# RG-LRU gates of a hybrid trunk: one 64-row product per 64-channel block in place of two zero-padded 128-row products

## The chip, the cores and the metric

One core of one Trainium2 chip runs the program. The metric is the device time of one execution in microseconds (us), as the median of several runs. PE is the matrix engine (TensorE), PEld its weight loads, ACT the ScalarE, DVE the VectorE, POOL the GpSimd engine, SP the engine whose queue issues most DMAs. Lnnn is a line of the kernel before.

## What is computed

Two layers of a streaming-encoder trunk over 256 tokens of width 1024. Each layer has a SwiGLU half-step, a mixer, a second SwiGLU half-step and an input embedding, each followed by a layer norm. The mixer projects x once and feeds three branches (RG-LRU, GLA, FoX). The change lies in the two gates of the RG-LRU branch, which has 512 channels in 8 blocks of 64:

```python
def rg_lru(x, wa, ba, wx, bx, lam):
    xb = xf.reshape(bsz, seq, LRU_BLOCKS, LRU_BLOCK)
    r = jax.nn.sigmoid(jnp.einsum('bsnc,ncd->bsnd', xb, wa.astype(f32)).reshape(bsz, seq, width) + ba.astype(f32))
    i = jax.nn.sigmoid(jnp.einsum('bsnc,ncd->bsnd', xb, wx.astype(f32)).reshape(bsz, seq, width) + bx.astype(f32))
    log_a = -LRU_C * r * jax.nn.softplus(-lam.astype(f32))
    a = jnp.exp(log_a)
    mult = jnp.sqrt(-jnp.expm1(2.0 * log_a))
    h = linear_scan(a, mult * (i * xf))
    return h.astype(x.dtype)
```

## The kernel before, in words

Weights stream from memory in pieces (`Weights.prefetch`, L183). For a piece the SP queue issues a DMA into `raw`, ACT rounds it into `whi` (L201) and DVE takes the rest into `wlo` (L202). Up to 8 pieces are held (`R_MAIN`), and a piece that PE has finished with is freed, which issues the next two. Every product with a streamed weight is three products of rounded parts (L305 to L307, L317 to L319).

All instructions are issued in the order of the program text, and each engine runs its own in that order. In the mixer (L527) the matrix units are run one after the other by `run` (L909): `run(unit, new chains)` first lets every chain in progress take one more step, up to its next `yield`, and then issues the unit's products. So the small chains of the three branches are laid between the units by hand:

- `run(lambda: unit_ay(1), lru(0))` starts `lru(0)`, the gates of the first 256 channels; `run(lambda: b_both(3, 1), lru(1))` starts `lru(1)`, those of the other 256.
- `unit_bq` and then `unit_cq(0)` follow. With `unit_cq(0)` the chain `gla_states` starts (products at L747, DVE copies at L756).
- Before `unit_k(0)` the chain `fox_forget` takes its transposes (L646), which read the tile `fcat` that DVE wrote at L634 to L639.
- Before `unit_cq(1)` the chain `gla_out` starts (products at L784, which read `gs`).

`lru(i)` (L684) does the gate products (L691), four sigmoids on ACT (L695), two tanh (L698) and two exp (L700), then `yield`s to its DVE steps. A tile of 256 channels stands on 128 partitions: column half `j` of `xc` holds 128 channels (two blocks) by 256 tokens. `wa` holds for each gate `w` and each pair of blocks a 128x128 matrix that is zero off its two 64x64 blocks. One PSUM tile (bank) holds one gate for both `j`. A float32 product is two passes on PE, each with its own weight load. There are 8 PSUM banks in one pool (`psp`), given out and given back in program order.

`gla_states` (L747), `gla_out` (L784) and `fox_attend` (L830) already use products of 64 rows, with the two halves in two banks.

Of the kernel before, what the change touches and what calls it, by code (L numbers as in the profile page):

```python
# [13 lines left out]
AF = mybir.ActivationFunctionType  # L14
# [3 lines left out]
P = 128  # L18
# [5 lines left out]
DEPTH = 2  # L24
# [116 lines left out]
V_CW, V_CB, V_BA, V_BX, V_LAM, NV = 0, 4, 5, 6, 7, 8  # L141


def constants():
    p = np.arange(P)
    ident = np.eye(P)
    suffix = (p[:, None] > p[None, :]) & (p[:, None] // 64 == p[None, :] // 64)
    prefix = p[:, None] <= p[None, :]
    ones = np.ones((P, P))
    chunk = p[:, None] // 64 == np.arange(2)[None, :]  # L150

    head = p[:, None] % 8 == np.arange(8)[None, :]
    keys, queries = p[:, None] < 24, (p[:, None] >= 32) & (p[:, None] < 56)
    cf = np.concatenate([ident, suffix, prefix, ones, chunk, head & queries, head & keys, -1.0 * keys, queries], 1).astype(np.float32)
    mask = np.where(p[None, :] <= p[:, None], 0.0, -1e30)
    cb = np.concatenate([ident, mask], 1).astype(np.float32)
    return cf, cb
# [74 lines left out]
def build(tc, a, out):  # L232
# [15 lines left out]
    def nm(s):  # L248
        count[0] += 1
        return f"{s}_{count[0]}"  # L250

    def ps():
        return psp.tile([P, 512], F32, tag="ps", name=nm("ps"))

    def work(n=512, dt=F32):
        return wk.tile([P, n], dt, tag="w", name=nm("w"))
# [4 lines left out]
    V, S, G, TE = nc.vector, nc.scalar, nc.gpsimd, nc.tensor  # L261

    def load(dst, src):
        nc.sync.dma_start(dst, src)

    def tt(out, in0, in1, op):
        return V.tensor_tensor(out=out, in0=in0, in1=in1, op=op)  # L267

    def stt(out, in0, scalar, in1, op0, op1):
        return V.scalar_tensor_tensor(out=out, in0=in0, scalar=scalar, in1=in1, op0=op0, op1=op1)  # L270
# [256 lines left out]
    def mixer(l, turn):  # L527
# [4 lines left out]
        wa = mt([P, 2, 4, P], F32, "wa")  # L532
# [3 lines left out]
        v = lambda kind, j: vec[:, (l * NV + kind) * 4 + j:(l * NV + kind) * 4 + j + 1]  # L536
# [22 lines left out]

        steps(b_steps((0, 1), 0), BT, turn, BA)  # L560
        W.hold = False
        load(wa, a["lru"][:, l])
        load(wg2, a["wg2"][l])
        load(ng, a["ng"][l, :].partition_broadcast(P))
        load(bf, a["bf"][l, :].partition_broadcast(P))
# [92 lines left out]
        def yt():  # L658
            y = mt([P, 4, 2, T], F32R, "y", 2)
            return y, y[:, :, 0, :], y[:, :, 1, :]  # L660


        ya = yt()
        js = [slice(j * T, (j + 1) * T) for j in range(2)]
# [19 lines left out]
        def lru(i):  # L684
            xc = lru_t["xc", i]
            r, ix, th = work(), work(), work()
            gates = []
            for w in range(2):
                o = ps()
                for j in range(2):  # L690
                    TE.matmul(o[:, js[j]], lhsT=wa[:, w, 2 * i + j, :], rhs=xc[:, js[j]], start=True, stop=True)  # L691
                gates.append(o)
            for w, dst in ((0, r), (1, ix)):
                for j in range(2):
                    S.activation(dst[:, js[j]], gates[w][:, js[j]], AF.Sigmoid, bias=v(V_BA + w, 2 * i + j))  # L695
            cs = [lruc[:, l * 4 + 2 * i + j:l * 4 + 2 * i + j + 1] for j in range(2)]
            for j in range(2):
                S.activation(th[:, js[j]], r[:, js[j]], AF.Tanh, scale=cs[j])  # L698
            for j in range(2):
                S.activation(r[:, js[j]], r[:, js[j]], AF.Exp, scale=cs[j])  # L700
            yield
            tt(ix, ix, xc, ALU.mult)

            tt(xc, r, r, ALU.mult)
            stt(th, xc, 1.0, th, ALU.add, ALU.mult)
            yield
            S.activation(th, th, AF.Sqrt, scale=-1.0)
            yield
            tt(ix, ix, th, ALU.mult)
            for j in range(2):  # L710
                V.tensor_tensor_scan(out=xc[:, js[j]], data0=r[:, js[j]], data1=ix[:, js[j]], initial=0.0, op0=ALU.mult, op1=ALU.add)
            tt(xc, xc, lru_t["ga", i], ALU.mult)
            yield
            hi, lo = (x[:, 2 * i:2 * i + 2, :] for x in ya[1:])
            xc3 = xc.rearrange("p (j c) -> p j c", j=2)
            S.activation(hi, xc3, AF.Copy)
            yield
            tt(lo, xc3, hi.bitcast(F32), ALU.subtract)
# [15 lines left out]


        yb = yt()
        rows = [slice(0, 64), slice(64, 128)]

        def gla_states():
            kd, dec = gla["kd"], gla["dec"]  # L740
# [174 lines left out]
        run(lambda: unit_ax(1), gla_decays())  # L915
        run(lambda: unit_ay(0), fox_forget(), gla_gate())
        run(lambda: unit_ay(1), lru(0))
        run(lambda: b_both(3, 0))
        run(lambda: b_both(3, 1), lru(1))
        run(unit_bq)  # L920
        run(lambda: unit_cq(0), gla_states())
# [182 lines left out]
    for l in range(DEPTH):  # L1104
        turn = ffn(l, 1, 0, hp, turn)
        W.close()
        sctx.close()
        gb, chains = mixer(l, turn)
        sctx, hp = open_scope(l + 1)
        turn = merge_out(l, gb, chains)  # L1110
        turn = ffn(l, 2, 2, hp, turn)
        turn = ple(l, turn, l == DEPTH - 1)
# [5 lines left out]
def lay_out(x, p, ffn1_w_up, ffn1_w_down, ln1_g, ln1_b, w_in, conv_w, conv_b, lru_wa, lru_ba, lru_wx, lru_bx,  # L1118
            lru_lambda, gla_w_g2, gla_b_g, gla_norm_g, fox_b_f, w_branch, w_out, ln2_g, ln2_b, ffn2_w_up,
            ffn2_w_down, ln3_g, ln3_b, ple_w_proj, ple_w_gate, ple_b_gate, ln4_g, ln4_b):  # L1120
    ws = {k: np.asarray(v) for k, v in locals().items()}
    f = np.float32
    parts = ((C_BK + 256, 512), (C_BK + 784, 512), (C_BK + 768, 16), (C_CF, 8), (C_BK, 256), (C_CV, 512))
    ws["tm"] = np.concatenate([ws["w_in"][..., c:c + n] for c, n in parts], -1)
    wu = np.empty(SIZE, f)
    for key, name, index, r0, rows, c0, cols, off in PIECES:
        block = ws[name][index][r0:r0 + rows]
        if "gu" in key[0]:
            block = np.concatenate([block[:, c0:c0 + 256], block[:, FF + c0:FF + c0 + 256]], -1)
        else:  # L1130
            block = block[:, c0:c0 + cols]
        block = block.reshape(rows // P, P, cols)
        wu[off:off + rows * cols].reshape(P, rows // P, cols)[...] = block.transpose(1, 0, 2)
    m = {"wu": wu}
    m["x"] = ws["x"].reshape(T, D)
    m["xT"] = ws["x"].reshape(T, KD, P).transpose(2, 1, 0).reshape(P, KD * T)
    m["pT"] = ws["p"].reshape(DEPTH, T, 2, P).transpose(3, 0, 2, 1)
    m["lnp"] = np.stack([ws[f"ln{i}_{c}"][l] for l in range(DEPTH) for i in range(1, 5) for c in "gb"])
    vec = np.empty((DEPTH, NV, 4, P), f)
    vec[:, :4] = ws["conv_w"].reshape(DEPTH, 4, 4, P)  # L1140
    for i, k in enumerate(("conv_b", "lru_ba", "lru_bx", "lru_lambda")):
        vec[:, 4 + i] = ws[k].reshape(DEPTH, 4, P)
    m["vec"] = vec.transpose(3, 0, 1, 2).reshape(P, DEPTH * NV * 4)
    lru = np.zeros((P, DEPTH, 2, 4, P), f)
    for w, k in enumerate(("lru_wa", "lru_wx")):
        for j in range(8):
            h = slice((j % 2) * 64, (j % 2) * 64 + 64)
            lru[h, :, w, j // 2, h] = ws[k][:, j].transpose(1, 0, 2)
    m["lru"] = lru
    wg2 = np.zeros((DEPTH, P, 256), f)  # L1150
    wg2[:, :16] = ws["gla_w_g2"]
    wg2[:, 32] = ws["gla_b_g"]
    m["wg2"] = wg2
    m["ng"] = ws["gla_norm_g"]
    m["bf"] = ws["fox_b_f"]
    m["bg"] = ws["ple_b_gate"]
    m["cf"], m["cb"] = constants()
    return {f"in_{k}": np.ascontiguousarray(v) for k, v in m.items()}
# [11 lines left out]
```

## Time and profile before

| | |
|---|---|
| median of 3 runs | 1316.31 us (1315.8 to 1317.02) |
| profiled execution | 1317.07 us, of which the span of its instructions is 1315.3 us |
| granted TensorE clock | 0.996 of full speed over the span |
| busy, share of the span | PE 98%, PEld 86%, DVE 68%, ACT 54%, POOL 4% |
| moved by DMA | 245.47 MB, mean 187 GB/s |

Busy shares are averages over stages with different limits. How a stage is bound is read from the time lines of its engines and from the table of waits, which says for each wait what ended it.

### The profile page before, as it was taken

To read this page: it belongs to the slowest core of one execution; us is meant where nothing else is said; L and a number is where in the kernel's file an instruction comes from. 1 tells how busy PE (TensorE), PEld (TensorE's weight loads), DVE (VectorE), ACT (ScalarE), POOL (GpSimd) and SP (SyncE) were. 2 spreads that over 40 slices of the span, in tenths; PEclk is the share of its full clock that TensorE was granted. 3 is DMA by queue.
4 is the path that set the end of the run, shared out by engine and by line. 5 is a ranking of instruction groups with operands and counts; after the bars stand their busy time and mean duration, and the time that the engine had idled before them with its cause. 6 is when DMAs were issued, how large, how long until landed. Compare 5 with 4: busy or idle time off the path is not lost. (4 is left out here: it accounts for less than half of the span.)

```text
span 1315.3 us, 19952 instructions
## 1 busy us (share of the span) xinstructions
PE 1287.2 (98%) x7892; PEld 1134.0 (86%) x7892; DVE 888.6 (68%) x1200; ACT 703.9 (54%) x1001; POOL 46.5 (4%) x42
## 2 busy tenths in 40 slices
PE   8999999999999999999999999999999999999996
PEld 7888888999999888887778888899999988888885
DVE  6776675678658666667776667665876586666676
ACT  6655545975445455554345556359655444555541
POOL 0000000000011000000000000000000110000000
PEclk9999999999999999999999999999999999999998
DMA  8865746446556465574555557463454655555731
GB/s 268 286 195 192 242 144 209 142 146 197 168 196 208 132 204 193 188 238 158 177 192 191 191 188 250 134 227 123 158 193 156 195 194 169 189 186 190 254 129 71
DMA packets 70061, 245.47 MB, mean 187 GB/s; under 512 B 8144, under 2 KB 8784, under 8 KB 69968
## 3 DMA queue, kind: packets, MB, share of 16 engines
q1 hardware_dynamic: 69680, 243.81, 56.2%
q8 instruction: 62, 1.02, 0.3%
q10 hardware_dynamic: 288, 0.39, 0.1%
q14 instruction: 31, 0.25, 0.1%
HBM read 243.12 MB, written 1.05 MB: 186 GB/s over the span
## 5 line engine op out<-in xcount | busy, mean ns | idle before, releaser
L202 DVE TENSOR_TENSOR wlo<-raw,whi 128x1024 fp32r<-128x1024 f32 (+2 forms) x442 | 538.6, 1228 | 252.5 <-ACT whi L201 251.3
L201 ACT ACTIVATE whi<-raw 128x1024 fp32r<-128x1024 f32 (+2 forms) x442 | 457.2, 1044 | 217.2 <-PE ps L318 80.7
L340 PE MATMUL ps<-XX,whi 128*128 128x512 f32 x1050 | 373.2, 393 | 0.0
L341 PE MATMUL ps<-XX,wlo 128*128 128x256 f32 x1200 | 312.5, 281 | 0.0
L341 PEld LDWEIGHTS ps<-XX,wlo 128*128 128x128 f32 x1200 | 226.0, 188 | 12.7 <-DVE wlo L202 0.2
L340 PEld LDWEIGHTS ps<-XX,whi 128*128 128x128 f32 x1050 | 196.9, 188 | 40.0
L317 PE MATMUL ps<-XX,whi 128*128 128x256 f32 x688 | 196.6, 286 | 5.9 <-ACT whi L201 5.9
L319 PE MATMUL ps<-XX,wlo 128*128 128x256 f32 x688 | 193.0, 281 | 0.0
L318 PE MATMUL ps<-XX,whi 128*128 128x256 f32 x688 | 193.0, 281 | 0.0
L305 PE MATMUL ps<-whi,hh 128*128 128x512 f32 x368 | 145.3, 395 | 2.5 <-ACT hh L276 2.5
L307 PE MATMUL ps<-whi,hl 128*128 128x512 f32 x368 | 144.1, 392 | 0.0
L306 PE MATMUL ps<-wlo,hh 128*128 128x512 f32 x368 | 143.2, 389 | 0.0
L345 ACT ACTIVATE w<-ps 128x256 f32<-128x256 f32 x150 | 57.3, 382 | 157.6 <-PE ps L343 157.6
L305 PE MATMUL ps<-whi,XX 128*128 128x512 f32 (+2 forms) x360 | 140.6, 391 | 0.0
L307 PE MATMUL ps<-whi,XX 128*128 128x512 f32 (+2 forms) x360 | 137.6, 382 | 1.1 <-DVE XX L267 1.1
L306 PE MATMUL ps<-wlo,XX 128*128 128x512 f32 (+2 forms) x360 | 137.5, 382 | 0.0
L317 PEld LDWEIGHTS ps<-XX,whi 128*128 128x128 f32 x688 | 130.3, 189 | 8.1 <-ACT whi L201 5.9
L318 PEld LDWEIGHTS ps<-XX,whi 128*128 128x128 f32 x688 | 130.4, 189 | 0.1
L319 PEld LDWEIGHTS ps<-XX,wlo 128*128 128x128 f32 x688 | 130.2, 189 | 0.2 <-DVE wlo L202 0.2
L267 DVE TENSOR_TENSOR w<-ps,w 128x256 f32<-128x256 f32 (+1 forms) x159 | 69.1, 435 | 76.4 <-ACT w L345 76.4
L307 PEld LDWEIGHTS ps<-whi,hl 128*128 128x128 f32 x368 | 69.0, 188 | 17.0 <-DVE hl L267 1.7
L305 PEld LDWEIGHTS ps<-whi,hh 128*128 128x128 f32 x368 | 69.1, 188 | 16.4 <-ACT hh L276 4.0
(171 smaller groups left out, 1371.1 us busy)
## 6 DMA issues: line engine op xcount, KB each, us to landing
raw<-in_wu SPq DMA_DIRECT2D x430, 512.0 KB, 4.2
gb<-in_lnp SPq DMA_DIRECT2D x16, 512.0 KB, 6.1
raw<-in_wu SPq DMA_DIRECT2D x8, 280.0 KB, 5.2
xr<-in_xT SPq DMA_DIRECT2D x4, 256.0 KB, 5.0
raw<-in_wu SPq DMA_DIRECT2D x4, 256.0 KB, 5.2
XR<-in_x SPq DMA_DIRECT2D x1, 1024.0 KB, 7.5
wa<-in_lru SPq DMA_DIRECT2D x2, 512.0 KB, 4.0
w<-in_bg SPq DMA_DIRECT2D x4, 256.0 KB, 5.0
```

The costliest lines, as they stand in the source:

```text
L201: self.nc.scalar.activation(hi[:, c], raw[:, c], AF.Copy)
L202: (lo or self.nc.vector).tensor_tensor(out=lw[:, c], in0=raw[:, c], in1=hi[:, c].bitcast(F32), op=ALU.subtract)
L267: return V.tensor_tensor(out=out, in0=in0, in1=in1, op=op)
L305: TE.matmul(o, lhsT=lh[:, k, c], rhs=hi[:, kk, :], start=start and kk == 0, stop=False)
L306: TE.matmul(o, lhsT=lh[:, k, c], rhs=lo[:, kk, :], start=False, stop=False)
L307: TE.matmul(o, lhsT=ll[:, k, c], rhs=hi[:, kk, :], start=False, stop=stop and kk == kt - 1)
L317: TE.matmul(o, lhsT=hi[:, kk, c], rhs=rhs[:, k, 0, :], start=start and kk == 0, stop=False)
L318: TE.matmul(o, lhsT=hi[:, kk, c], rhs=rhs[:, k, 1, :], start=False, stop=False)
L319: TE.matmul(o, lhsT=lo[:, kk, c], rhs=rhs[:, k, 0, :], start=False, stop=stop and kk == kt - 1)
L340: TE.matmul(o, lhsT=hi[:, k, :], rhs=both, start=k == 0, stop=False)
L341: TE.matmul(o[:, :T], lhsT=lo[:, k, :], rhs=XX[:, k, 0, :], start=False, stop=False)
L345: S.activation(lows[:, c], o[:, T:], AF.Copy)
```

## The change

Each 64-channel block now has its two 64x64 gate matrices side by side in one 64x128 matrix. For each column half `j` and each block `e` of it (even on partitions 0 to 63, odd on 64 to 127) one product contracts 64 rows and gives 128 outputs: gate r on PSUM partitions 0 to 63 and gate i on 64 to 127. Even blocks go to one bank, odd blocks to another. The products are four for one `lru` as before, but of 64 rows. Each sigmoid now covers 64 partitions, from `rows[w]` of bank `e` to `rows[e]` of the output, so there are eight of 64x256 where there were four of 128x256. The load of `wa` is half as large (its tile keeps its size, since `unit_k` uses the slot again), and `rows` is defined earlier.

```diff
-        load(wa, a["lru"][:, l])
+        load(wa[:, 0], a["lru"][:, l])
...
-            gates = []
-            for w in range(2):
-                o = ps()
-                for j in range(2):
-                    TE.matmul(o[:, js[j]], lhsT=wa[:, w, 2 * i + j, :], rhs=xc[:, js[j]], start=True, stop=True)
-                gates.append(o)
+            gates = [ps() for _ in range(2)]
+            for j in range(2):
+                for e in range(2):
+                    TE.matmul(gates[e][:, js[j]], lhsT=wa[rows[e], 0, 2 * i + j, :], rhs=xc[rows[e], js[j]], start=True, stop=True)
             for w, dst in ((0, r), (1, ix)):
                 for j in range(2):
-                    S.activation(dst[:, js[j]], gates[w][:, js[j]], AF.Sigmoid, bias=v(V_BA + w, 2 * i + j))
+                    for e in range(2):
+                        S.activation(dst[rows[e], js[j]], gates[e][rows[w], js[j]], AF.Sigmoid, bias=v(V_BA + w, 2 * i + j)[rows[e]])
...
-    lru = np.zeros((P, DEPTH, 2, 4, P), f)
+    lru = np.zeros((P, DEPTH, 4, P), f)
...
-            lru[h, :, w, j // 2, h] = ws[k][:, j].transpose(1, 0, 2)
+            lru[(j % 2) * 64:(j % 2) * 64 + 64, :, j // 2, w * 64:w * 64 + 64] = ws[k][:, j].transpose(1, 0, 2)
```

## Rows read from the trace of the kernel before

**Rows 1.** The page, its first part: busy time of the engines, share of the span, instructions.

```profile
PE 1287.2 (98%) x7892; PEld 1134.0 (86%) x7892; DVE 888.6 (68%) x1200; ACT 703.9 (54%) x1001; POOL 46.5 (4%) x42
```

**Rows 2.** The table of waits for PE alone, whole run: who waited for whom, us in total, times, longest.

```profile
PE ps L317 <- ACT whi L201: 5.9, 1, 5.9
...
PE ps L784 <- ACT whi L201: 2.6, 2, 1.3
...
PE ps L646 <- DVE fcat L639: 0.4, 2, 0.3
```

**Rows 3.** Windows: busy time of each engine in three stretches, with the granted clock and the DMA share. The first two are the stretch from the first `axp` copy to the `bq` copy in the mixer of layer 0 and of layer 1; the third follows it in layer 0.

```profile
core 0: us, PE busy (x) PEld busy (x) DVE busy (x) ACT busy (x) POOL busy (x), PEclk, DMA share, GB/s
235.40:276.50 41.10, 40.83 (x309) 37.62 (x308) 21.30 (x38) 40.71 (x57) 2.74 (x2) 1.00 0.38 117
887.50:929.50 42.00, 41.83 (x314) 38.52 (x313) 21.82 (x40) 41.60 (x57) 2.73 (x2) 1.00 0.36 119
276.50:285.10 8.60, 7.22 (x74) 6.52 (x76) 8.46 (x18) 4.93 (x6) 0.00 (x0) 1.00 0.37 124
```

**Rows 4.** Time line of ACT in layer 0: start, us, line, operation, count, and in brackets the idle time before it and what ended that.

```profile
234.37 1.06 ACT L201 ACTIVATE whi<-raw 128x1024 fp32r<-128x1024 f32 x1 [1.74 <-PE ps L318]
235.42 0.60 ACT L671 ACTIVATE axp<-ps 128x512 f32<-128x512 f32 x1
...
251.13 1.57 ACT L695 ACTIVATE w<-ps,vec 128x256 f32<-128x256 f32 x4
252.57 0.92 ACT L698 ACTIVATE w<-w,lruc 128x256 f32<-128x256 f32 x2
...
266.65 1.57 ACT L695 ACTIVATE w<-ps,vec 128x256 f32<-128x256 f32 x4
268.09 0.92 ACT L698 ACTIVATE w<-w,lruc 128x256 f32<-128x256 f32 x2
...
272.57 1.05 ACT L201 ACTIVATE whi<-raw 128x1024 fp32r<-128x1024 f32 x1
...
275.89 0.59 ACT L722 ACTIVATE bq<-ps 128x512 f32<-128x512 f32 x1
278.90 0.63 ACT L716 ACTIVATE y<-w 128x512 fp32r<-128x512 f32 x1 [2.42 <-DVE w L267]
```

**Rows 5.** Time line of DVE, the same columns: layer 0, and behind the last gap one row of layer 1.

```profile
264.75 0.69 DVE L267 TENSOR_TENSOR w<-w,tm 128x512 f32<-128x512 f32 x1
272.22 1.23 DVE L202 TENSOR_TENSOR wlo<-raw,whi 128x1024 fp32r<-128x1024 f32 x1 [6.78 <-ACT whi L201]
273.65 1.23 DVE L202 TENSOR_TENSOR wlo<-raw,whi 128x1024 fp32r<-128x1024 f32 x1 [0.20 <-ACT whi L201]
274.79 0.17 DVE L634 COPY s<-ps 128x16 f32<-128x16 f32 x1
...
276.07 0.17 DVE L639 CAST fcat<-s 128x16 bf16<-128x16 f32 x1
...
283.11 0.48 DVE L756 COPY gs<-ps 128x128 f32<-128x128 f32 x2
283.51 1.64 DVE L270 SCALAR_TENSOR_TENSOR gs<-gs,s,ps 128x128 f32<-128x128 f32 x6
...
926.71 1.23 DVE L202 TENSOR_TENSOR wlo<-raw,whi 128x1024 fp32r<-128x1024 f32 x1 [0.20 <-ACT whi L201]
```

**Rows 6.** Time line of PE around the transposes of `fcat`: layer 0, then layer 1.

```profile
275.74 0.28 PE L319 MATMUL ps<-XX,wlo 128*128 128x256 f32 x1
276.30 0.29 PE L646 MATMUL ps<-cb,fcat 128*128 128x128 bf16 x2 [0.27 <-DVE fcat L639]
...
929.36 0.28 PE L646 MATMUL ps<-cb,fcat 128*128 128x128 bf16 x2 [0.17 <-DVE fcat L639]
```

**Rows 7.** Groups of ACT instructions by line and shape (out<-in, count, busy us, mean ns of one).

```profile
L201 ACT ACTIVATE whi<-raw 128x1024 fp32r<-128x1024 f32 x430 | 449.3, 1055 | 211.0 <-PE ps L318 80.7 <-DMA raw<-in_wu 58.2 <-issue 28.3
...
L695 ACT ACTIVATE w<-ps,vec 128x256 f32<-128x256 f32 x16 | 6.3, 475 | 0.0
...
L578 ACT ACTIVATE w<-w 128x16 f32<-128x16 f32 x2 | 0.4, 216 | 0.0
```

**Rows 8.** Time line of PE around the gate products of `lru(0)` in layer 0 (the products take xc and wa; x8 are four products of two passes).

```profile
240.52 0.28 PE L318 MATMUL ps<-XX,whi 128*128 128x256 f32 x1
240.64 0.28 PE L319 MATMUL ps<-XX,wlo 128*128 128x256 f32 x1
240.75 1.89 PE L691 MATMUL ps<-w,wa 128*128 128x256 f32 x8
...
242.60 0.28 PE L318 MATMUL ps<-XX,whi 128*128 128x256 f32 x1
```

**Rows 9.** Time line of PE around the products of `gla_states` in layer 0 (16 float32 products of 64 rows and 64 columns, two passes each).

```profile
268.91 0.28 PE L319 MATMUL ps<-XX,wlo 128*128 128x256 f32 x1
...
269.12 1.10 PE L747 MATMUL ps<-gv,w 64*64 64x128 f32 x32
...
270.15 0.39 PE L317 MATMUL ps<-XX,whi 128*128 128x256 f32 x1
...
270.38 0.28 PE L318 MATMUL ps<-XX,whi 128*128 128x256 f32 x1
```

**Rows 10.** Time line of PE in `fox_attend` in layer 0: products of 64 rows and 128 columns, even and odd halves in two banks.

```profile
303.64 0.28 PE L830 MATMUL ps<-gv,qh 64*128 64x128 f32 x2
...
303.76 0.27 PE L830 MATMUL ps<-wa,ql 64*128 64x128 f32 x2
```

**Rows 11.** Windows of PE alone around one pause between the layers: us, busy time, granted clock (PEclk), DMA share.

```profile
652.24:655.65 3.41, 3.41 (x13) 0.50 0.28 84
648.80:652.24 3.44, 1.14 (x8) 1.00 0.47 155
```

**Rows 12.** The page, DMA issues: size and median us from issue to landing.

```profile
wa<-in_lru SPq DMA_DIRECT2D x2, 512.0 KB, 4.0
```

More of the change, by code (lines that the diff above doesn't have):

```diff
@@ L660, in yt @@
             return y, y[:, :, 0, :], y[:, :, 1, :]
+        rows = [slice(0, 64), slice(64, 128)]
         ya = yt()
@@ L736, in mixer @@
         yb = yt()
-        rows = [slice(0, 64), slice(64, 128)]
         def gla_states():
@@ L1143, in lay_out @@
     m["vec"] = vec.transpose(3, 0, 1, 2).reshape(P, DEPTH * NV * 4)
-    lru = np.zeros((P, DEPTH, 2, 4, P), f)
+    lru = np.zeros((P, DEPTH, 4, P), f)
     for w, k in enumerate(("lru_wa", "lru_wx")):
         for j in range(8):
-            h = slice((j % 2) * 64, (j % 2) * 64 + 64)
-            lru[h, :, w, j // 2, h] = ws[k][:, j].transpose(1, 0, 2)
+            lru[(j % 2) * 64:(j % 2) * 64 + 64, :, j // 2, w * 64:w * 64 + 64] = ws[k][:, j].transpose(1, 0, 2)
     m["lru"] = lru
```

## The prediction

> **What bounds the kernel now.** I read the page's busy times first: PE is busy for 1287.2 us of a span of 1315.3, so over the whole run the kernel is bound by products, and time that PE loses is not won back later [rows 1]. Taken alone this says that products should be cut. The second view, PE's waits, says what ends the little idle time that it has: after the start (5.9 us for the first weights) PE never waits long for a weight piece, but at two places in the mixer it waits for the small chains, at L646 for `fcat` from DVE and at L784 [rows 2]. Both lie shortly behind the changed lines, so I looked at that stretch by itself. In the 41.1 us from the first `axp` copy to the `bq` copy ACT is busy for 40.71 us, in layer 1 for 41.60 of 42.00, while DVE is busy for half of the time [rows 3]. ACT's average of 54% hides a stretch in which it is as full as PE.
>
> The time line of ACT shows how [rows 4]: from the copy at 235.42, which PE's product released, to the copy at 275.89 no idle time stands in brackets. Sigmoids, tanh, exp, table loads and the splitting of weights follow each other without a pause, and both `lru` calls lie in it (251.13 and 266.65). Nothing that ACT does there is waiting for PE: it works off a backlog. Now I follow who waits for the end of the backlog. DVE stands idle for 6.78 us and again for 0.20 us until ACT has split a weight piece (the one at 272.57 ends at 273.62; DVE starts at 273.65); in DVE's queue the `fcat` steps come right behind that piece, from 274.79 to 276.24 [rows 5]. PE issues its last product of `unit_cq(0)` at 275.74, could go on some 0.12 later, and starts L646 at 276.30 with idle time that `fcat` ends; in layer 1 the same happens at 929.36 [rows 6]. So the path that sets the time in this stretch is ACT's queue, then two DVE steps, then PE; PE reaches L646 about 0.4 us early in both layers.
>
> **The change part by part.** *Sigmoids.* Four instructions become eight in each `lru`. The elements per partition stay 256. An ACT row's time goes with those: 1055 ns for 1024, 475 for 256, 216 for 16 [rows 7]. No ACT row of this kernel covers fewer than 128 partitions, so the cost of a 64x256 sigmoid is bounded. From below: half the cost, which makes the eight as long as the four, +0; I see no reason for less, since the same elements are read. From above: 0.475 each with no overlap, 8 x 0.475 - 1.44 = +2.36 us for a call. Back to back, four take from 251.13 to 252.57, 1.44 us or 0.36 each [rows 4]. The nearest row is the sigmoid itself with half of the lanes idle, so I take the same 0.36: eight take 2.88, +1.44 us for a call. Two calls in a layer lie on the gap-free stretch, +2.88 us; two layers, **+5.76 us**.
>
> The Trainium skill, "ScalarE: Activation LUTs", section "What ACT_TABLE_LOAD costs", gives an activation with a pointer bias 280 ns + 0.833 ns for each element of a partition, less some 93 ns of overlap, with no term for partitions: an estimate of 0.40 us for each, +1.6 for a call and 6.4 in all. The row's 0.475 us and step of 0.36 are both below its 0.493 and 0.40, and the sum goes by the rows.
>
> *Who takes it up.* ACT has no gap in which to take it up, DVE's start at 273.65 is released by ACT, and PE's slack is 0.4 us but in the wrong place: PE waits for DVE already, so a later `fcat` moves L646 one for one, 276.30 to about 279.2. After that DVE is busy for 8.46 us of 8.60 up to the `gs` steps [rows 3], all behind `fcat` in its queue, so the start of L784, which waits for `gs` at 283.51 [rows 5], moves by the same 2.88. Weight pieces split on ACT also come 2.88 us later, but with eight pieces of 24 products at 0.12 us each PE holds some 22 us of work (an estimate), which covers that; if it didn't, the wait would fall into the same 2.88 us. From L784 on PE, ACT and DVE are late by the same amount, and nothing takes it back.
>
> *Products.* Before, `lru(0)` costs PE the time from the product at 240.64 to the second one behind it at 242.60, 1.96 us, less two ordinary steps of 0.115: 1.73 us, or 8 passes of 0.216 [rows 8]. After, there are again 8 passes of 256 columns, in two row halves. Do halves run at the same time? At L747 32 passes of 128 columns take 270.38 - 268.91 - 0.23 = 1.24 us; one after the other at half of 0.216 they would take 3.46. So four tiles do run together, 8 steps of 0.108 = 0.86, plus 0.38 us for entering and leaving the form [rows 9]. At L830 two halves of 64x128 last as long together, 0.28 us, as one alone, and the next pair starts 0.12 later [rows 10]. So I take 4 steps of 0.216 + 0.38 = 1.24 us, 0.49 less for a call, 1.96 us in all; the bounds are 0 (no overlap, with 0.38 more for the form: 1.5 us lost in all) and half of 1.73, 3.46 us gained in all. But all four calls lie ahead of the wait at L646 of their layer. What PE gains there, it waits longer at L646: **0**. If ACT were not late, the same holds, since PE already arrives early.
>
> *Banks.* A bank used to be read by two sigmoids, now by four, the last two of which are the seventh and eighth in the queue. Counting the banks in the order in which they are given back, `unit_cq(0)` gets the first of `lru(1)`'s two. Before, that was free after the second sigmoid, some 0.36 + 0.47 us behind 266.65, at 267.5, well ahead of the product at 270.15 [rows 9]. Now it is free after the seventh: 266.65 + 1.44 + 6 x 0.36 + 0.47 = 270.7. PE, a microsecond early, waits there, with L317 to L319 of `unit_cq(0)` and all units queued behind; its 5.85 us of products then end at 276.6, still ahead of 279.2. The wait is inside the other one and costs nothing by itself; were L646 not late it would cost about 0.3. For all other hand-overs of these banks PE has a microsecond or more.
>
> *DVE, queues, load.* DVE's steps of `lru` are unchanged in number; `kd` at 264.75 moves to about 266.9 at its end, ahead of the products at 268 that read it. The load of `wa` halves, one of 512 KB and 4.0 us in a layer [rows 12], in a place where DMA engines are busy for 0.36 to 0.38 of the time [rows 3] and nobody waits for it: 0. It stands in SP's queue where it stood.
>
> Sum: 5.76 + 0 + 0 + 0. The profiled execution's 1317.07 us (span 1315.3 and 1.77 around it) becomes 1322.8; it lies 0.76 above the median of the runs shown, so the median becomes 1316.31 + 5.76 = **1322.1 us**.
>
> **The rivals.** (a) *The half-height sigmoid costs half.* For it: no row shows one. Against: rows go with elements per partition. ACT's chain is then as long as before, PE's gain is waited away, and the time is 1316.3; a cost between the two gives 1318 to 1320. (b) *PE's gain reaches the end*: faster. The place is L646: if ACT's backlog were worked off before the piece that DVE waits for, PE's arrival would decide, and 1.96 us less makes 1314.4, with no cost for the form 1312.9. It begins to decide where ACT has 2.88 + 0.4 = 3.3 us of idle time between 235 and 272 to take the sigmoids up, and gives all from 4.3 us. Against it: ACT has 0.39 us [rows 3]. The Trainium skill's "TensorEngine Tiling (Array Packing)", section "Theoretical Speedup", promises up to 2x for a dimension of 64 or less; that is this rival's 1312.9. L747's 1.24 us for 3.46 agrees that tiles run together, so the speed-up on PE is likely there; it is its way to the end that I doubt. (c) *The sigmoids don't overlap*, for instance because two write one tile: 4 x 2.36 = 9.4, 1325.7. Against: four sigmoids before also write one tile by halves and do overlap. (d) *The clock falls.* PE was busy for 1.14 us of 3.44 at 648.80 and the next 3.41 us ran at 0.50, the lower level of 1.2 GHz [rows 11]. Here PE would stand for some 1.7 us at `unit_cq(0)` and some 2.6 at L646, either of which might do the same. 3.41 us at half the clock are 1.7 us of products; `unit_k(0)` behind L646 is followed by 1.3 us of idle time before L784 (2.6 us in two waits) [rows 2], so some 0.4 for a layer remains, 1322.9, or 1325.5 where it falls in a place without cover.
>
> **How the numbers follow.** Forecast 0.68, (a) 0.13 (0.02 of it at a cost between the two that can be told), (b) 0.05, (c) 0.07, (d) 0.07. A measurement of this kernel can tell about 0.2%, 2.6 us, from no change. Slower by more than that: the forecast, (c), (d) and 0.02 of (a), 0.84; the same: the rest of (a), 0.11; faster: 0.05. The range takes in (c), (d) and that part of (a), 1318.5 to 1325.8, and leaves out (b) and the rest of (a). The forecast's own band is 1321 to 1323, from a sigmoid step of 0.32 to 0.40.
>
> **What would show it.** In the changed kernel's time line of ACT, eight sigmoids from start to the tanh in 2.9 us, and no idle time before them; the wait of PE at L646 grown from 0.3 to some 2.6 us in each layer, with DVE's `fcat` named; a wait at the first product of `unit_cq(0)`; the gate products in about 0.9 us from first to last start. Wrong would be: sigmoids of 0.18 us step, L646 reached without a wait, or idle time of ACT in the stretch.

## The result, and the profile after

| | before | after |
|---|---|---|
| median of the runs taken together, us | 1316.59 (4 runs, 1315.8 to 1317.02) | 1326.14 (4 runs, 1325.76 to 1326.96) |
| profiled execution, its span, us | 1317.07, 1315.3 | 1325.76, 1324.0 |
| granted clock, mean of the span | 0.996 | 0.993 |

The change costs time: ratio 1.0082, 95% interval [1.0068, 1.0096], which is 9.0 to 12.6 us; the medians lie 9.55 us apart. The sign and the path were forecast, the size was not: 1322.1 had been expected, and 1326.14 lies outside 1318.5 to 1325.8.

In the changed kernel the gate products are L693, the sigmoids L697, tanh L700, exp L702; later lines move by one or two (L784 is L785).

The page's busy times, against [rows 1]:

```profile
PE 1287.4 (97%) x7892; PEld 1133.1 (86%) x7892; DVE 888.2 (67%) x1200; ACT 713.0 (54%) x1017; POOL 46.6 (4%) x42
```

ACT has 16 instructions more and 9.1 us more of busy time. The other busy times are where they were, so the loss shows as idle time of PE: span less busy time is 28.1 us before and 36.6 after. PE's waits, to be held against [rows 2]:

```profile
PE ps L317 <- ACT w L697: 6.3, 2, 3.2
PE ps L317 <- ACT whi L201: 5.7, 1, 5.7
...
PE ps L646 <- DVE fcat L639: 2.8, 2, 1.4
PE ps L785 <- ACT whi L201: 2.6, 2, 1.3
```

The first row is new: the first product of `unit_cq(0)` waits twice, once in a layer, for a sigmoid that still reads its bank. The wait at L646 grew from 0.4 to 2.8 us; that at L785 is as before. Time line of ACT in layer 0, against [rows 4]:

```profile
249.80 3.90 ACT L697 ACTIVATE w<-ps,vec 64x256 f32<-64x256 f32 x8
253.73 0.91 ACT L700 ACTIVATE w<-w,lruc 128x256 f32<-128x256 f32 x2
254.65 1.28 ACT L702 ACT_TABLE_LOAD   x1
255.95 0.91 ACT L702 ACTIVATE w<-w,lruc 128x256 f32<-128x256 f32 x2
...
267.80 3.89 ACT L697 ACTIVATE w<-ps,vec 64x256 f32<-64x256 f32 x8
271.71 0.91 ACT L700 ACTIVATE w<-w,lruc 128x256 f32<-128x256 f32 x2
```

Eight sigmoids take 253.73 - 249.80 = 3.93 us, a step of 0.49, where four had taken 1.44 at a step of 0.36. A call costs 2.49 us more, four calls 9.96. No idle time stands in brackets: the sigmoids are not waiting, they follow each other more slowly. One of them lasts as long as a full one did (mean 470 ns, [rows 7] had 475):

```profile
L697 ACT ACTIVATE w<-ps,vec 64x256 f32<-64x256 f32 x32 | 15.0, 470 | 0.6
```

Half of the partitions, then, cost the same; and the 0.11 us by which two neighbours used to overlap (0.475 - 0.36) are gone. Downstream, DVE in layer 0, against [rows 5]:

```profile
275.82 1.23 DVE L202 TENSOR_TENSOR wlo<-raw,whi 128x1024 fp32r<-128x1024 f32 x1 [9.24 <-ACT whi L201]
277.39 1.23 DVE L202 TENSOR_TENSOR wlo<-raw,whi 128x1024 fp32r<-128x1024 f32 x1 [0.34 <-ACT whi L201]
278.54 0.17 DVE L634 COPY s<-ps 128x16 f32<-128x16 f32 x1
...
279.81 0.17 DVE L639 CAST fcat<-s 128x16 bf16<-128x16 f32 x1
```

The chain is the one of before: ACT's piece, DVE's `wlo`, the `fcat` steps, and behind them PE. Read off the two traces it comes 3.7 us later (`fcat` at 279.81 against 276.07, and L785 at 287.28 where L784 had 283.54), but this trace is 1.33 us ahead of that of before at the first sigmoid (249.80 against 251.13). From there to `fcat` it takes 5.1 us more, and two calls give 2 x 2.49 = 4.98. Time line of PE, against [rows 6, 8, 9]: the gate products, the start of `unit_cq(0)`, and L646 in both layers.

```profile
239.41 0.27 PE L319 MATMUL ps<-XX,wlo 128*128 128x256 f32 x1
239.62 1.14 PE L693 MATMUL ps<-w,wa 64*128 64x256 f32 x8
240.68 0.39 PE L317 MATMUL ps<-XX,whi 128*128 128x256 f32 x1
240.91 0.28 PE L318 MATMUL ps<-XX,whi 128*128 128x256 f32 x1
...
271.25 0.38 PE L317 MATMUL ps<-XX,whi 128*128 128x256 f32 x1 [3.17 <-ACT w L697]
...
280.04 0.29 PE L646 MATMUL ps<-cb,fcat 128*128 128x128 bf16 x2 [1.37 <-DVE fcat L639]
...
938.48 0.28 PE L646 MATMUL ps<-cb,fcat 128*128 128x128 bf16 x2 [1.38 <-DVE fcat L639]
```

The products did get cheaper: 240.91 - 239.41 = 1.50 us, less two ordinary steps of 0.115, is 1.27 us for a call against 1.73, so 0.46 less. And PE's clock, by windows of all engines behind the new pause (columns as in [rows 3]):

```profile
268.00:271.20 3.20, 0.08 (x4) 0.00 (x0) 0.00 (x0) 3.08 (x7) 0.00 (x0) 1.00 0.43 151
272.00:275.40 3.40, 3.40 (x18) 3.40 (x18) 0.00 (x0) 3.37 (x6) 0.00 (x0) 0.50 0.00 0
...
930.80:934.20 3.40, 3.40 (x18) 3.40 (x17) 0.00 (x0) 3.37 (x5) 0.00 (x0) 0.50 0.02 5
```

PE stood for 3.2 us, and 3.4 us of `unit_cq(0)` then ran at 0.50, the lower level; the last row shows the same in layer 1. That takes 1.7 us of product time, and PE still came 1.37 us too early for `fcat`.

The books close to within a microsecond: PE's idle time at the bank and at L646 is 6.3 + 2.8 = 9.1 us, the low clock takes 2 x 1.7 = 3.4, together 12.5; less the 0.4 us of wait that was there before and the 4 x 0.46 = 1.84 that the products gave, 10.3 us, for 9.96 of added ACT time and 9.55 measured.

### The profile page after: what moved, and what is told of

It is laid out like the page before. It is cut to its first block, busy times and chain, and to the rows that moved or that the text cites. A ratio compares the mean times of both kernels' runs of the same rounds, so it can differ in the third digit from the quotient of the medians.

```text
span 1324.0 us, 19970 instructions
## 1 busy us (share of the span) xinstructions
PE 1287.4 (97%) x7892; PEld 1133.1 (86%) x7892; DVE 888.2 (67%) x1200; ACT 713.0 (54%) x1017; POOL 46.6 (4%) x42
## 5 line engine op out<-in xcount | busy, mean ns | idle before, releaser
L306 PEld LDWEIGHTS ps<-wlo,hh 128*128 128x128 f32 x368 | 69.1, 188 | 14.7
```

Source lines behind the costliest of these rows:

```text
L306: TE.matmul(o, lhsT=lh[:, k, c], rhs=lo[:, kk, :], start=False, stop=False)
```

## Experiments

Theory after the result: ACT's queue sets L646, and the eight sigmoids cost 0.49 us each because neighbours on different partitions don't overlap. Rivals: PE's new form or the bank wait is what costs; or the overlap is lost to the half height, to the shift from one partition half to the other, or to the turn of the bank. The first four runs tell these apart.

**Halves by turns, before's products.** Each sigmoid of before is cut into its two partition halves; input and output stand on the same partitions, both halves read one bank.

```diff
-                    S.activation(dst[:, js[j]], gates[w][:, js[j]], AF.Sigmoid, bias=v(V_BA + w, 2 * i + j))
+                    for e in range(2):
+                        S.activation(dst[rows[e], js[j]], gates[w][rows[e], js[j]], AF.Sigmoid, bias=v(V_BA + w, 2 * i + j)[rows[e]])
...
```

> The kernel before with its full 128-row products, but each sigmoid cut into two of 64 partitions, from rows e of a bank to the same rows e of the output (no shift), upper and lower half by turns, both halves out of the same bank. In the changed kernel eight sigmoids take 3.93 us (a step of 0.49) where four took 1.44 (0.36). If it is the half height or the turn from one half to the other that keeps two sigmoids from overlapping, the step is 0.49 here too and the run is as slow as the changed kernel, +9 to +10 us against before (about 1326). If it is the shift of partitions between source and output, or the turn from bank to bank, the step is 0.36, eight take 2.9 and the run is at +5.8 us (1322.4). If the 64-row products cost the time, +0.

Measured: 1324.9 us against 1314.62 of the kernel before on that chip, ratio 1.0076 [1.0061, 1.0091], some 10 us: the whole loss of the change, with PE's products, banks and the load as before. ACT and PE:

```profile
249.58 3.87 ACT L697 ACTIVATE w<-ps,vec 64x256 f32<-64x256 f32 x8
253.47 0.91 ACT L700 ACTIVATE w<-w,lruc 128x256 f32<-128x256 f32 x2
```

```profile
PE ps L646 <- DVE fcat L639: 8.7, 2, 4.4
...
PE ps L317 <- ACT w L697: 1.4, 2, 0.7
```

```profile
279.60:283.00 3.40, 3.25 (x16) 3.26 (x17) 3.30 (x8) 0.96 (x3) 0.00 (x0) 0.53 0.42 154
```

Eight in 253.47 - 249.58 = 3.89 us, the step of the changed kernel, without a shift between partitions. PE's waits grew by 8.3 us at L646 and 1.4 at the bank, and the 2.6 us at L784 are gone. The last fence, a window of layer 0 (columns as in [rows 3]), says why: behind its 4.4 us of idle time at L646 PE's clock fell to the lower level, and about 1.7 us of product time that this costs in each layer (in layer 1 the stretch 938.00 to 941.40 ran at 0.58) take the place of the wait at L784. In all that is 8.3 + 1.4 - 2.6 + 3.4 = 10.5 us, for 4 x 2.45 = 9.8 us of added ACT time. With nothing else changed, the cause is on ACT alone.

**The bank turned at each sigmoid.** Before, with the four in the order r, i, r, i.

```diff
-            for w, dst in ((0, r), (1, ix)):
-                for j in range(2):
+            for j in range(2):
+                for w, dst in ((0, r), (1, ix)):
```

> The kernel before with its four full sigmoids in the order r, i, r, i, so that each one reads another bank and writes another tile than the one ahead of it. If the turn from bank to bank prevents overlap, the four take 1.9 us instead of 1.44 and the run is 1.8 us longer. Else no change: 1.44 and 1316.6.

Measured in a single run: 1313.99 us; the four take 1.44 us again:

```profile
249.88 1.57 ACT L695 ACTIVATE w<-ps,vec 128x256 f32<-128x256 f32 x4
251.32 0.92 ACT L698 ACTIVATE w<-w,lruc 128x256 f32<-128x256 f32 x2
```

Neither a turn of the bank nor one of the output tile costs the overlap.

**Halves in groups, before's products.** The halves of the first run, but all four even ones first, then all four odd ones.

```diff
-            for w, dst in ((0, r), (1, ix)):
-                for j in range(2):
-                    S.activation(dst[:, js[j]], gates[w][:, js[j]], AF.Sigmoid, bias=v(V_BA + w, 2 * i + j))
+            for e in range(2):
+                for w, dst in ((0, r), (1, ix)):
+                    for j in range(2):
+                        S.activation(dst[rows[e], js[j]], gates[w][rows[e], js[j]], AF.Sigmoid, bias=v(V_BA + w, 2 * i + j)[rows[e]])
...
```

> As the run with full products and halved sigmoids, but the four lower halves first and then the four upper ones; source and output always stand on the same partitions, so one step of seven turns. Turn theory: six or seven steps of 0.36 and one of 0.49, eight in 3.0 us, +1.57 a call and +6.3 us, 1322.9. Half-height theory: step 0.49, 1326.

Measured: 1321.7 us, ratio 1.0057 [1.0037, 1.0077]. ACT:

```profile
249.71 1.55 ACT L697 ACTIVATE w<-ps,vec 64x256 f32<-64x256 f32 x4
...
251.28 1.56 ACT L697 ACTIVATE w<-ps,vec 64x256 f32<-64x256 f32 x4
252.86 0.91 ACT L700 ACTIVATE w<-w,lruc 128x256 f32<-128x256 f32 x2
```

Four halves on the same partitions last 1.55 us from first start to last end, as four full ones do (1.57): they overlap, a step of 0.36. Between the groups nothing overlaps: the second starts at 251.28, where the first ended at 251.26. So half height costs the full 0.36 and no more; the turn to other partitions costs 0.13 more (1.57 us from start to start of the groups, for 4 x 0.36 = 1.44). The second group loses another 0.14 to the tanh behind it, which covers all partitions: eight take 252.86 - 249.71 = 3.15 us, 1.71 more than four had.

**The changed kernel in groups.** Its sigmoids in the order bank, gate, column half. Here the source partitions turn with the gate, the output partitions only with the bank.

```diff
-            for w, dst in ((0, r), (1, ix)):
-                for j in range(2):
-                    for e in range(2):
+            for e in range(2):
+                for w, dst in ((0, r), (1, ix)):
+                    for j in range(2):
```

> The changed kernel with the same eight sigmoids in another order: first the four of the even blocks (output partitions 0 to 63, one bank), then the four of the odd ones. Only one of the seven steps turns to other output partitions; two more turn the source's partitions. If the half height by itself prevents overlap, all steps stay at 0.49 and the time at 1326. If the turn of partitions does, five or six of the eight steps fall to 0.36: 3.1 to 3.3 us for eight, +1.7 to +1.85 a call against before, 1323.4 to 1324.

Measured: 1323.12 us, ratio 1.0072 [1.0053, 1.009]; eight take 3.41 us, 1.97 more than four had. The four pairs of sigmoids of one call, a row for each:

```profile
250.58 0.83 ACT L697 ACTIVATE w<-ps,vec 64x256 f32<-64x256 f32 x2
251.42 0.84 ACT L697 ACTIVATE w<-ps,vec 64x256 f32<-64x256 f32 x2
252.28 0.83 ACT L697 ACTIVATE w<-ps,vec 64x256 f32<-64x256 f32 x2
253.13 0.83 ACT L697 ACTIVATE w<-ps,vec 64x256 f32<-64x256 f32 x2
```

Within a pair two of 0.47 take 0.83, so they overlap. Between pairs there is a gap of 0.01 to 0.03 us, also between the first and the second, where only the source partitions turned. The changed kernel's own order keeps the source's partitions through one gate and turns the output's at every instruction, and there no two overlap either: a turn of one of the two is enough. One thing is not told apart: the bias stands on the output's partitions in all these runs and turns with it, so what was shown of the output holds for output and bias together.

The next four ask what PE's gain is worth.

**Products on the diagonal.** Before's four sigmoids, and eight products of 64x64 in the two corners of the matrix unit, without the zeros.

```diff
...
-                for j in range(2):
-                    TE.matmul(o[:, js[j]], lhsT=wa[:, w, 2 * i + j, :], rhs=xc[:, js[j]], start=True, stop=True)
...
+            for x in range(2):
+                for j in range(2):
+                    for e in range(2):
+                        w = x ^ e
+                        TE.matmul(gates[w][rows[e], js[j]], lhsT=wa[rows[e], w, 2 * i + j, rows[e]], rhs=xc[rows[e], js[j]], start=True, stop=True)
...
```

> The kernel before with its sigmoids untouched, but the gate products cut into eight of 64 rows and 64 columns that write only the diagonal blocks, two at a time on the two halves of the array, never both into one bank. PE's part of the change without ACT's. The products should take from first to last start about 0.75 us as in the changed kernel, 0.49 us less for each call. If what PE gains ahead of L646 is waited away there, the time stays at that of before within 0.8 us, and PE's wait at L646 grows from 0.4 to 1.4 us in each layer. If PE's gain reaches the end, it is 2 us faster (about 0.15%).

Measured: 1315.72 us against 1315.43, ratio 0.9999 [0.999, 1.0007]. But the wait at L646 was gone, which was not expected, and the products show why the run doesn't tell the theories apart:

```profile
240.64 0.27 PE L319 MATMUL ps<-XX,wlo 128*128 128x256 f32 x1
240.85 1.94 PE L693 MATMUL ps<-w,wa 64*64 64x256 f32 x16
242.72 0.38 PE L317 MATMUL ps<-XX,whi 128*128 128x256 f32 x1
242.94 0.28 PE L318 MATMUL ps<-XX,whi 128*128 128x256 f32 x1
```

Sixteen passes, two at a time, are eight steps again, and the form has its own price: 242.94 - 240.64 = 2.30 us where [rows 8] have 1.96, 0.34 more for a call. The expectation counted a gain that this edit doesn't have. All that the run shows is that 0.7 us of PE for a layer, 1.4 in all, went under. The 0.4 us of wait at L646 hold a part of it. Another 0.4 us came off the second wait (L784, here L783; 2.6 us before):

```profile
PE ps L783 <- ACT whi L201: 2.2, 2, 1.3
```

And PE's slack at L646 is some 0.3 us larger than its recorded wait: by the starts in [rows 6] it could have gone on at 275.86 and went on at 276.30, 0.44 us, of which 0.27 are recorded; layer 1 has 0.33 and 0.17. That makes 1.1 of the 1.4 us, and the rest lies within the interval.

**The changed products alone.** The gain by itself, with the sigmoids in their old form.

```diff
...
-                    TE.matmul(o[:, js[j]], lhsT=wa[:, w, 2 * i + j, :], rhs=xc[:, js[j]], start=True, stop=True)
...
+                    TE.matmul(gates[e][:, js[j]], lhsT=wa[rows[e], 0, 2 * i + j, :], rhs=xc[rows[e], js[j]], start=True, stop=True)
...
```

> The kernel before with the changed kernel's four gate products of 64x128 a call and two banks by block, but the sigmoids in their old form: four of 128x256, each over the whole height of a bank, so that PE's part of the change is there and ACT's is not (the lanes of the two gates are mixed by it, the amount of work is that of before; the load of wa stays 512 KB). PE's cost of a call, from the last ordinary product ahead of the gate products to the second one behind them, is 1.96 us less two ordinary steps of 0.115 = 1.73 in before, and 1.50 less two = 1.27 in the changed kernel: 0.46 less a call, 0.92 a layer, 1.84 us in all. Theory (ACT's queue, then DVE's fcat steps, set the start of L646; PE's gain is waited away there): time within 0.8 us of before, the sigmoids at steps of 0.36, the wait of PE for fcat at L646 up from 0.4 us in two to about 2.2 in two. Rival (PE is the bound, since it is busy for 98% of the span): 1.8 us less than before, and no longer a wait at L646.

Measured: 1315.43 us against 1314.75, ratio 1.0006 [0.9998, 1.0015]. The rival's 1.8 us less is outside the interval. PE's waits:

```profile
PE ps L782 <- ACT whi L201: 2.6, 2, 1.3
PE ps L646 <- DVE fcat L639: 2.1, 2, 1.1
```

The wait at L646 grew by 1.7 us, from 0.4 to 2.1: the gain of 1.84 us stands there as idle time, as expected. A single trace is good to some half a microsecond here (the run with the order r, i, r, i, whose work is that of before, has 1.0 us at L646), so it is the time that excludes the rival, and the wait says where the gain went.

**One gate fewer on ACT**, with the old products, and then with the changed ones.

```diff
-            for w, dst in ((0, r), (1, ix)):
+            for w, dst in ((0, r),):
...
-            tt(ix, ix, xc, ALU.mult)
+            tt(ix, r, xc, ALU.mult)
```

> The kernel before without the sigmoids of gate i: two of 128x256 a call instead of four, and the product with xc takes gate r in gate i's place (so the result lacks that gate; the gate products on PE are all there). ACT's queue gets 0.72 us shorter a call, 1.44 a layer. Theory (ACT's queue sets L646, with PE only 0.3 to 0.4 us early): fcat comes up to 1.44 us sooner, PE's slack at L646 of 0.4 us a layer is gone, from then on PE decides: 0.3 to 1.0 us less in all, no wait at L646. Rival (sigmoids are cheap beside what the queue really waits for, and the changed kernel lost its time at the bank wait): no difference, the wait at L646 stays.

> Both edits of its two neighbours: the changed kernel's products on PE (0.46 us less a call) and only two full-height sigmoids a call (0.72 us less on ACT), so that gate i is left out of the result. Theory (two queues, the later one decides at L646): PE can now come 0.92 us + its old slack of 0.3 to 0.4 sooner a layer and ACT 1.44, so PE's gain shows: 2.0 to 2.8 us less than before in all, though it was worth nothing with four sigmoids. Rival (PE's gain is lost at another place, whatever ACT does): no more than the run with one gate and the old products gives.

Measured against 1314.75: 1312.09 us, ratio 0.9978 [0.9969, 0.9987], with the old products, and 1311.53, 0.9979 [0.997, 0.9987], with the changed ones. The first is 2.9 us faster by the ratio (2.7 by medians), as much as the 4 x 0.72 = 2.88 us that ACT gave and more than the 0.3 to 1.0 expected. The second is 2.8 us faster by the ratio (3.2 by medians). That is about the 2.0 to 2.8 expected, but not for the reason given: the gate alone brings as much, and the changed products add nothing clear of noise. The waits say why. Old products:

```profile
PE ps L784 <- ACT whi L201: 0.4, 2, 0.2
```

Changed products:

```profile
PE ps L782 <- ACT whi L201: 2.4, 2, 1.3
```

PE has two waits behind the same backlog in a layer, at L646 and, seven microseconds on, at L784. (For L784 the table names ACT's `whi`, while its products read `gs`, which DVE writes at the same moment; which of the two ends the wait is not settled.) I had counted the first alone as its slack. With ACT shorter by 1.44 us a layer, DVE's whole queue comes forward and both shrink: of 0.4 + 2.6 = 3.0 us of recorded wait 0.4 is left, at L784, and L646 is no longer in the table. With PE faster as well, its gain passes L646 and is waited away at L784 instead: 0.4 + 1.84 = 2.2 us, and 2.4 are there. The rival of the last run (PE's gain is lost at another place) was right.

**The waits put one unit later**: `fox_forget` yields once more ahead of L646, and `gla_out` starts with `unit_k(1)`; in before, in the diagonal form and in the changed kernel.

```diff
+            yield
...
-        run(lambda: unit_cq(1), gla_out())
-        run(lambda: unit_k(1))
+        run(lambda: unit_cq(1))
+        run(lambda: unit_k(1), gla_out())
```

> The kernel before with the two places at which PE waits for the small chains moved one unit later: one more yield ahead of the transposes of fcat (L646), and gla_out started with unit_k(1) instead of unit_cq(1). Products and sigmoids are those of before. If ACT's queue, then DVE, set the time at these two places, PE's waits there (0.4 and 1.3 us in each layer) go and the run is 2 to 3.4 us faster. If PE's idle time there is made up for later anyway, or comes back at the new places, 0.

> The diagonal 64x64 products with the sigmoids of before, and the two waits moved one unit later as well. If the place of the waits decides whether PE's gain counts, it counts here: 2 us less than the run with the later waits alone, 4 to 5.4 us less than before. If PE's gain is worth nothing for another reason (the entering and leaving of the form, a stall elsewhere), the same time as the run with the later waits alone.

> The changed kernel with the two waits moved one unit later. ACT's queue is still 5 us longer in each layer. The waits at the transposes and at gla_out should go; the wait of unit_cq(0) for the seventh sigmoid (3.2 us in each layer, of which PE's earlier arrival is 1) stays, and the slower clock behind it (1.5 us in each layer), which the wait at the transposes covered, now counts. Against before: 2 x (2.2 + 1.5) - 3.4 = +4 us, 5 to 6 us faster than the changed kernel. If ACT's longer queue holds PE back everywhere in the mixer and not at these places alone, it stays at +9.

Measured against 1315.43: before 1319.31, ratio 1.0031 [1.002, 1.0041]; diagonal 1316.34, 1.0018 [1.0007, 1.003]; changed kernel 1330.4, 1.0118 [1.0104, 1.0133]. All three missed against before: nothing was won, and the changed kernel lost 15 us instead of 4. Its waits:

```profile
PE ps L317 <- ACT w L698: 6.3, 2, 3.2
...
PE ps L827 <- DVE fQ L273: 5.1, 2, 3.2
```

The idle time left L646 and L785 (2.8 + 2.6 us) and came back a unit later, 5.1 us in front of `fox`'s own products, with the low clock behind it where no wait covers it (columns as in [rows 3]):

```profile
306.60:310.00 3.40, 3.17 (x28) 2.61 (x28) 3.37 (x8) 2.53 (x3) 0.99 (x1) 0.50 0.72 254
310.00:313.40 3.40, 3.40 (x21) 3.28 (x19) 3.00 (x6) 0.00 (x0) 1.60 (x1) 0.50 0.60 181
```

In layer 0 that costs 3.3 us of product time, in layer 1 1.7 (0.91 and 0.58 of full speed in two such windows from 966.0 on). These 5.0 us and the 9.55 of the change make 14.6, about the 15 measured; this is a sum read off one trace, and no run tests it by itself.

In before, moved in this way, the idle time does the same: 3.9 us where 0.4 + 2.6 had stood at the old places.

```profile
PE ps L826 <- DVE fQ L273: 3.9, 2, 2.0
```

Its profiled execution was the shortest of twelve (1313.98, the others 1317.29 to 1322.64), with a granted clock of 0.995 over the span where the others have 0.990 to 0.993. A difference of 0.003 is 4 us, so the lower clock can account for most of the median's loss; where the other runs lost it no trace shows, and that stays open. The diagonal form with the later waits is 3.0 us below before with the later waits by medians. 2 us had been expected there, from a gain that its products don't have, so this stays open too; the times of the two kernels overlap widely (1314.6 to 1321.1 and 1313.98 to 1322.64).

**A shorter queue on ACT**, to see what the theory is good for: each gate as 0.5 + 0.5 tanh(x/2). In the time line of ACT above no table load stands between sigmoid and tanh, but one of 1.28 us does between tanh and exp in every call; with tanh throughout, the hope was for one load fewer.

```diff
-                    S.activation(dst[:, js[j]], gates[w][:, js[j]], AF.Sigmoid, bias=v(V_BA + w, 2 * i + j))
+                    S.activation(dst[:, js[j]], gates[w][:, js[j]], AF.Tanh, scale=0.5, bias=v(V_BA + w, 2 * i + j))
...
-                S.activation(th[:, js[j]], r[:, js[j]], AF.Tanh, scale=cs[j])
+                S.activation(th[:, js[j]], r[:, js[j]], AF.Tanh, scale=cs[j], bias=cs[j])
...
-                S.activation(r[:, js[j]], r[:, js[j]], AF.Exp, scale=cs[j])
+                S.activation(r[:, js[j]], r[:, js[j]], AF.Exp, scale=cs[j], bias=cs[j])
...
-            tt(ix, ix, xc, ALU.mult)
+            stt(ix, ix, 1.0, xc, ALU.add, ALU.mult)
...
```

> The kernel before with its old products and four full-height activations a call, but each gate as 0.5 + 0.5 tanh(x/2): tanh, then tanh and exp with a bias, so that one table load of 1.28 us fewer stands in each call; the factors one half go into the constants, the product with xc and the root, and the result is the reference's. ACT's queue gets 1.28 us shorter a call, 2.56 a layer. The run with one gate took 1.44 us a layer off ACT and was 2.9 us faster, the two waits of PE at L646 and L784 falling from 0.4 + 2.6 to 0.4 us. Theory (ACT's queue sets L646 and, through DVE, L784, and PE could come 1.5 us sooner a layer and no more): these two waits disappear, the time falls by the whole 3.0 us and stops there though ACT gives 5.1. Rival (the time follows ACT's queue without a bound from PE): 5.1 us less. Second rival (what helped the run with one gate was something else than ACT's time, such as banks that are free sooner): no change.

Measured: 1311.43 us against 1314.79, ratio 0.9972 [0.9962, 0.9983], 2.2 to 5.0 us less: faster than both kernels. ACT in layer 0:

```profile
265.33 1.57 ACT L695 ACTIVATE w<-ps,vec 128x256 f32<-128x256 f32 x4
266.77 1.10 ACT L698 ACTIVATE w<-w,lruc 128x256 f32<-128x256 f32 x2
267.76 1.10 ACT L700 ACTIVATE w<-w,lruc 128x256 f32<-128x256 f32 x2
268.74 1.06 ACT L201 ACTIVATE whi<-raw 128x1024 fp32r<-128x1024 f32 x1
```

The load is gone, but tanh and exp with a bias take 1.10 for two where they took 0.92: from the first activation to the next piece 268.74 - 265.33 = 3.41 us, against 271.14 - 266.65 = 4.49 in the trace of before, 1.08 less for a call and 4.3 in all. So "follows ACT without a bound" is 4.3 here, not the 5.1 expected, and the time alone doesn't tell it from 3.0. The waits speak for the bound: neither L646 nor L784 is left among PE's waits, and PE arrives at L646 without idle time:

```profile
275.60 0.28 PE L319 MATMUL ps<-XX,wlo 128*128 128x256 f32 x1
275.72 0.29 PE L646 MATMUL ps<-cb,fcat 128*128 128x128 bf16 x2
```

## Why the prediction was right in its path and wrong in its size

- **ACT's queue, then `fcat`, then PE**: right. The chain of [rows 4 to 6] is there after the change, later by what ACT got, and the first run (halves by turns) brings the whole loss by ACT alone. In five kernels the time follows what ACT got or gave: by medians, one gate fewer gave -2.7 us for -2.88, halves in groups +7.1 for 4 x 1.71 = 6.8, the changed kernel in groups +8.5 for 4 x 1.97 = 7.9, halves by turns +10.3 for 9.8, the change +9.55 for 9.96. One row was misread, without effect: the gap that PE's product ended stands ahead of the piece at 234.37, not of the copy at 235.42.
- **The size of the sigmoids: the step that failed.** It was "I take the same 0.36: eight take 2.88, +1.44 us for a call", and it measured 3.93 and +2.49. The choice of row was right for what it claimed (a half-height sigmoid does cost 0.36 behind one on the same partitions), but a step is made by two neighbours, and in the change no two neighbours write the same partitions. The upper bound of the same paragraph, "0.475 each with no overlap", +2.36, was the value, and 4 x 2.36 = 9.4 the result. The range ended at that case's 1325.7 without the 0.01 to 0.03 us between two that don't overlap (0.49 is not 0.475), and so the time fell just outside, by 0.34 us; the median of before had also moved, by 0.28, from 1316.31 to 1316.59. A range half a microsecond wider would have held the time, and the step of 0.36 would have been as wrong.
- **Rival (c)** had the right mechanism and price at a chance of 0.07, and the reason that it was given, two sigmoids that write one tile, was the wrong one to test: it was refuted from the trace of before, and with it went the rival. The turn of the bank or tile costs nothing (r, i, r, i), the turn of partitions does (groups). The Trainium skill, "ScalarE: Activation LUTs", section "What ACT_TABLE_LOAD costs", has back-to-back activations overlap by some 93 ns; the rows agree with 0.11 us on the same partitions and show none at a turn, and where the two differ the rows decide.
- **Rival (a)**, half the height at half the price: refuted, 470 ns for 64 partitions.
- **Products**: 0.49 us less for a call was predicted, 0.46 measured; that it is worth nothing was right (the changed products alone: 1.0006, and 1.7 us more of wait at L646).
- **Rival (b)**, that PE's gain would reach the end if ACT gave up 3.3 us: its place was not the only one. Behind L646 the same queue is waited for again at L784, and there the gain is lost with ACT shorter by 1.44 us a layer than before. By the recorded waits PE's slack is 1.5 us a layer (3.0 in two), not 0.4.
- **Banks**: the wait at `unit_cq(0)` for the seventh sigmoid was foreseen, at a length of some 1.7 us; it is 3.17 us long, since the seventh sigmoid ends 3.45 us behind the first of its call (267.80 to 271.25) where 2.6 had been counted, and the call itself starts later by the 2.49 us that the first call took more. It lies inside the lateness of L646, and with the slower clock behind it, it is why the wait at L646 grew to 1.4 us a layer and not to the 2.6 that the prediction named as a sign.
- **Rival (d)**, the clock: it does fall, behind the bank wait, in both layers, and costs nothing where it falls, since PE then only waits less at L646. The other place that the prediction named, behind L646, is seen in the halves by turns: there the clock fell behind a wait of 4.4 us, and the idle time at L784 paid for 2.6 of the 3.4 us that it cost in two layers, which leaves the 0.4 a layer of the prediction. In the moved version the fall behind the bank again only shortens a later wait (3.2 us are left at L827 in layer 0); the fall behind L827 has no cover, and makes 5.0 of the 15 us.
- **DVE, load of `wa`, weight pieces**: nothing to see in the waits, as forecast.

## What to carry to other kernels

Where one engine's queue runs without a gap and another waits for its end, count the instructions of the full engine and the step from one to the next, not the work of the engine that shows 98%: the saving on PE here went into a wait almost whole, 1.7 us of 1.84. Each half of an ACT instruction that is split by partitions costs what the whole did (0.36 us a step even in groups), and 0.13 more at each turn to other partitions; where the split can't be avoided, group the halves that stand on the same partitions. And add up all waits that hang on the same queue before saying how much slack an engine has.

## Not expected of the hardware

- Two ACT instructions overlap (0.36 us from start to start for 0.47 us each, 256 elements) only where source and output stand on the partitions of the one before; a turn of the source alone (the groups of the changed kernel), of the output alone (the changed kernel) or of both (halves by turns) makes the step 0.47 to 0.50. The bias stood on the output's partitions throughout. A turn of bank or tile doesn't (0.356 to 0.372).
- Activations of 64 partitions take what those of 128 take: 470 against 475 ns.
- A bias as a pointer added 0.09 us to each tanh and exp (1.10 for two, 0.92 without).
- Eight 64x64 products on the diagonal, two at a time, take PE 0.34 us longer than four zero-padded ones of 128 rows; four of 64x128, two at a time, 0.46 us less.
